# First pair of feature tiles of each FFN by plain products, and what goes with it

## The chip, the cores and the metric

The kernel runs on one core of a Trainium2 chip. Its time is the device time of one execution in microseconds (us). The kernel before takes 1070.05 us, the median of 3 runs (1069.14 to 1070.71).

## The reference

One layer of a streaming encoder on a sequence of 512 positions, 1024 features, in float32:

```
x = x + 0.5 * swiglu(rms_norm(x, ffn1_norm), w_gate1, w_up1, w_down1)     # FFN 1
x = x + mixer(rms_norm(x, mix_norm))                                      # SSD scan and chunked attention
x = x + 0.5 * swiglu(rms_norm(x, ffn2_norm), w_gate2, w_up2, w_down2)     # FFN 2
return rms_norm(x, final_norm)
# swiglu(h, g, u, d) = (silu(h @ g) * (h @ u)) @ d ; g, u: 1024 x 2816, d: 2816 x 1024
```

The change touches the two FFNs (and one buffer of the attention).

## The kernel before

Everything lies transposed: features on the 128 partitions, the 512 positions on the free axis. x is 8 tiles of 128 x 512, the 2816 inner features are 22 tiles, taken in 11 pairs. Each float32 product is made of three TensorE matmuls on operands that are split in a high and a low part (high x high, high x low, low x high); ScalarE (ACT) makes the high part of a weight tile and VectorE (DVE) the low one (`usplit`, lines 284 and 286).

Gate and up of one pair are computed together by a scheme of seven products in place of eight (the Strassen-Winograd kind): `wgu[d, 0..3]` are four blocks of weights (gate and up, each over four of the eight input tiles, 512 KB a block), x has four quarters (input tiles 0 to 3 and 4 to 7, positions LO = 0 to 255 and HI = 256 to 511), and the products P1 to P7 take a block or a sum of blocks by a quarter or a sum of quarters. One product is a *unit*: 2 feature tiles x 4 input tiles x 3 = 24 matmuls of 256 columns (line 445). P1, P2 and P4 take plain weights. P5, P6, P3 and P7 take sums of blocks, which the DMAs make: P5's buffer is loaded with block 2 by a plain DMA (line 318) and block 3 is added by an accumulating DMA that GpSimd (POOL) issues (line 321); after P5's split block 0 is added for P6, after that split block 1 for P3. For P7 block 2 is added onto P1's buffer. So a pair takes four plain and four accumulating loads of 512 KB. The buffer of sums, `view(d)`, exists twice (tile s40), that of plain weights, `raw`, four times.

The sums of x (`XCombos`) are made on DVE: `weigh` multiplies x by the norm weights into `xw`, `sum1`, `sums23` and `sum4` make the sums, `parts1`, `parts23`, `parts4` split them in high and low; `base` splits plain x.

1/rms isn't in x: it is put in after the products. `rstd_begin` sums squares (accumulated in `acc` by `add_squares`, square on ACT, add on DVE line 170) over partitions with ones matmuls and runs some 15 tiny DVE operations; `rstd_both` spreads the result to all partitions with two matmuls and copies it to `rs[0]` (1/rms) and `rs[1]` (-0.5/rms). After P3, gate is multiplied by `rs[0]`, then SiLU, then by up (after P4), and the product is split for the down matmul. The down matmul's output is multiplied by `rs[1]` and added to x (`add`, lines 483 and 484).

The order of the work is written out in `program()`: units of pairs 0 and 1 interleaved, then for d = 2 to 10: P5(d), P1(d), P3(d-1), P4(d-1), P6(d), P2(d), P7(d), and after pairs 4 and 8 a block of down matmuls ("D"), the third block at the end. After each unit one step of a generator (`early1`, `early2`) does a piece of the sums of x and of 1/rms. `ws.get()` hands out the weights: it splits `look` units ahead and starts the DMAs of the next 8 units by the lead that each one has. The instructions of each engine run in an order fixed at compile time; a scheduler may place an instruction earlier than the text does when its inputs and buffers are free in its own reckoning, and the text's order is its priority. Each engine, and each queue that issues DMAs (SP, POOL), runs its own list in order.

In the attention four tiles `kz0` to `kz3` of 128 x 512 hold a part of the keys. In FFN 2 the last three output tiles are finished by halves of the positions (`last2`).

Of the kernel before, what the change touches and what calls it, by code (L numbers as in the profile page):

```python
# [38 lines left out]
def hybrid_block(ctx: ExitStack, tc, xT, par, wgu1, wd1, win, wdt, wv, wo, rbt, wgu2, wd2, out):  # L39
# [83 lines left out]
    class Stream:  # L123
# [40 lines left out]
    def add_squares(acc, src, first):  # L164
# [72 lines left out]
    GROUPS = {22: 8, 36: 4, 40: 4, 44: 4}  # L237
# [63 lines left out]

    def ffn_weights(wgu, wd, n_last=0):
# [20 lines left out]
        for step in program(n_last):  # L323
            if step[0] == "P":
# [3 lines left out]
                if p == "P1":  # L328
# [28 lines left out]
    class XCombos:  # L357


        def __init__(self, wcol):  # L360
# [3 lines left out]
            self.b1, self.t1 = [[two() for _ in range(2)] for _ in range(2)]  # L364
            self.b2, self.t23 = [[two() for _ in range(4)] for _ in range(2)]
# [35 lines left out]
        def split(self, dst, src):  # L401
            d = [p.rearrange("p (a b) -> p a b", a=2) for p in dst]
# [15 lines left out]
        def moving(self, p, k):
            if p == "P1":
                return self.half(self.b1, k)  # L420
            if p == "P5":
                return self.half(self.t1, k)
            if p == "P4":
                return self.half(self.t4, k)
            t, h = {"P2": (self.b2, LO), "P3": (self.b2, HI), "P6": (self.t23, HI), "P7": (self.t23, LO)}[p]
            return [a[:, h] for a in t[k]]

    def ffn(xc, early, after, last=None, n_last=0):
# [4 lines left out]
        early = early(rs)  # L433

        def run(p, d):
# [22 lines left out]
            elif p == "P3":  # L458
                V.tensor_tensor(out=e["b"], in0=e["H"], in1=e["b"], op=ALU.add)
                e["s"] = []  # L460
                for t, h in (("a", LO), ("b", HI)):
# [3 lines left out]
                    S.activation(out=s, in_=e[t], func=AF.Silu)  # L465
                    e["s"].append(s)
            elif p == "P4":

                q = HSLOT[d % 4]
                th, tl = [wide_tile(group(q))[:, i - group(q):i - group(q) + 2] for i in (q, q + 2)]  # L470
# [6 lines left out]
                for j in range(2):  # L477
                    hh[2 * d + j], hl[2 * d + j] = th[:, j], tl[:, j]
                del st[d]

        def add(o, ps):
            t = sb("fh", [P, SEQ], bufs=2)
            V.tensor_tensor(out=t, in0=ps, in1=rs[1], op=ALU.mult)  # L483
            V.tensor_tensor(out=x[:, o], in0=x[:, o], in1=t, op=ALU.add)

        pss = {}
        for i, step in enumerate(program(n_last)):
            if step[0] == "P":
                run(*step[1:])
                next(early, None)  # L490
# [40 lines left out]
    for k in range(4):  # L531
        xc1.base(x[:, k], k)
# [8 lines left out]

    def early1(rs):
        ws.look = 2
# [3 lines left out]
        for k in range(4):  # L547
            xc1.weigh(x[:, k], k)
        yield
        ws.look = 3  # L550
        xc1.sum1()
        xc1.parts1()
        for k in range(4, 8):
            xc1.weigh(x[:, k], k)
        yield
        xc1.sums23()
        yield
        for k in range(4):
            xc1.parts23(k)
        yield  # L560
        acc = sb("acc", [P, SEQ])
        for k in range(4):
            add_squares(acc, x[:, k], k == 0)
        yield
        xc1.sum4()
        xc1.parts4()
        for k in range(4, KD):
            add_squares(acc, x[:, k], False)
        dg, _ = rstd_begin(acc, D)
        yield  # L570
# [3 lines left out]
        yield  # L574
        rstd_both(rs, dg)
# [222 lines left out]
    def do_qk(j, n, ps):  # L798
# [260 lines left out]
    for o in range(KD):  # L1059
# [7 lines left out]
        if o < 4:  # L1067
            xc3.weigh(x[:, o], o)
        add_squares(accs[1], x[:, o], o == 0)
        if o == 4:  # L1070
            xc3.sum1()
        if o >= 5:
            xc3.weigh(x[:, o - 1], o - 1)

    def early2(rs):
        xc3.weigh(x[:, KD - 1], KD - 1)
        yield
        xc3.parts1()
        yield
        xc3.sums23()  # L1080
        yield
        for k in range(4):
            xc3.parts23(k)
        yield
        dg, _ = rstd_begin(accs[1], D)
        yield
        xc3.sum4()
        xc3.parts4()
        yield
        yield  # L1090
        rstd_both(rs, dg)
        yield
# [12 lines left out]
    def last2(hh, hl, rsm):  # L1105
# [115 lines left out]
```

## Time and profile before

| | us |
|---|---|
| median of 3 runs | 1070.05 |
| the profiled execution | 1071.2 |
| its span | 1069.5 |
| granted TensorE clock, mean | 0.987 |

In the profile, PE is the matmul engine, PEld its weight loads, DVE VectorE, ACT ScalarE, POOL GpSimd, SP the queue that issues plain DMAs. A row of the timeline has the start, the duration, the engine, the line of the kernel, the operation, output and input tiles, shapes, the number of merged instructions, and in brackets the idle time before it and what ended it. A row of groups has count, busy us and mean ns of one, then the idle time before and its releasers.

### The profile page before, as it was taken

What the parts mean: (1) busy time and instruction counts of PE and PEld (TensorE: products, weight loads), DVE (VectorE), ACT (ScalarE), POOL (GpSimd) and SP (SyncE); (2) the same over time, 40 slices, a digit from 0 to 9 for tenths busy, and PEclk for the clock granted to TensorE, in tenths of its full rate; (3) what the DMA queues carried; (4) which work ended last, traced back from release to release, by engine and by line L of the source; (5) the groups of instructions that cost most, each with busy time, mean ns of one, the idle gap of its engine ahead of it and who ended that gap; (6) DMA issues with size and microseconds to landing.
All of it is one profiled execution on the core that took longest, in us unless ns stands there. A gap on an engine that the chain in (4) does not pass through costs nothing.

```text
span 1069.5 us, 16508 instructions
## 1 busy us (share of the span) xinstructions
PE 1027.5 (96%) x6494; PEld 923.7 (86%) x6494; DVE 760.4 (71%) x1252; ACT 551.1 (52%) x876; POOL 137.0 (13%) x157
## 2 busy tenths in 40 slices
PE   7799999999999999999999999998899999999995
PEld 6799889998899877878888778888898899989985
DVE  6787655675466878988867999787675477645765
ACT  6565432563244546755666876656462155423543
POOL 2111100110010003323201111110110011100000
PEclk9799999999999999999999999999999999999997
DMA  9789754986453322222232232757895388853612
GB/s 300 155 178 220 199 136 104 212 223 172 118 113 95 118 76 73 79 60 78 60 99 80 79 99 80 181 114 170 203 237 140 99 183 210 219 134 98 137 46 79
DMA packets 44126, 145.92 MB, mean 136 GB/s; under 512 B 4624, under 2 KB 7952, under 8 KB 44048
## 3 DMA queue, kind: packets, MB, share of 16 engines
q1 hardware_dynamic: 29136, 95.69, 26.7%
q0 software_dynamic: 12672, 46.14, 25.1%
q10 hardware_dynamic: 2240, 3.02, 1.0%
q8 instruction: 51, 0.84, 0.3%
q14 instruction: 27, 0.22, 0.1%
HBM read 142.74 MB, written 2.10 MB: 135 GB/s over the span
## 4 chain that ended last, share of the span: by engine, by line
PE 66%; DMA 11%; DVE 11%; issue 6%; ACT 5%; POOL 0%; SPq 0%; DVEq 0%; ACTq 0%; POOLq 0%
PE mm L445 16%; PE mm L154 12%; PE mm L155 12%; PE mm L156 12%; PE aux L445 10%; DMA s<-wgu 10%; DVE fs L625 2%; DVE xw L286 2%; ACT xw L284 2%; DVE wlo L104 1%; PE aux L985 1%; PE aux L749 0%; DMA raw<-wd 0%; ACT s L475 0%; PE aux L1007 0%
## 5 line engine op out<-in xcount | busy, mean ns | idle before, releaser
L445 PE MATMUL mm<-s,xw 128*128 128x256 f32 x2112 | 272.8, 287 | 16.1 <-ACT fu L453 8.2
L445 PEld LDWEIGHTS mm<-s,xw 128*128 128x128 f32 x2112 | 264.4, 196 | 19.7 <-ACT fu L453 9.5
L445 PE MATMUL aux<-s,xw 128*128 128x256 f32 x1584 | 202.7, 285 | 8.1 <-ACT xw L284 6.6
L445 PEld LDWEIGHTS aux<-s,xw 128*128 128x128 f32 x1584 | 196.5, 193 | 9.5 <-ACT xw L284 6.8
L102 ACT CAST whi<-raw 128x512 fp32r<-128x512 f32 (+1 forms) x178 | 105.9, 603 | 154.7 <-PE mm L155 126.6
L104 DVE TENSOR_TENSOR wlo<-raw,whi 128x512 fp32r<-128x512 f32 (+1 forms) x178 | 122.5, 694 | 48.5 <-ACT whi L102 47.6
L286 DVE TENSOR_TENSOR xw<-raw,xw 128x1024 fp32r<-128x1024 f32 x88 | 107.5, 1221 | 52.1 <-ACT xw L284 52.0
L155 PE MATMUL mm<-s,whi 128*128 128x512 f32 x366 | 142.7, 390 | 0.0
L154 PE MATMUL mm<-s,whi 128*128 128x512 f32 x366 | 142.5, 390 | 0.0
L156 PE MATMUL mm<-s,wlo 128*128 128x512 f32 x366 | 142.4, 389 | 0.0
L284 ACT CAST xw<-raw 128x1024 fp32r<-128x1024 f32 x88 | 92.1, 1048 | 89.4 <-PE mm L445 35.6
L284 ACT CAST xw<-s 128x1024 fp32r<-128x1024 f32 x66 | 69.1, 1048 | 132.6 <-PE aux L445 53.9
L286 DVE TENSOR_TENSOR xw<-s,xw 128x1024 fp32r<-128x1024 f32 x66 | 80.6, 1221 | 54.9 <-ACT xw L284 54.8
L154 PE MATMUL mm<-xw,whi 128*128 128x512 f32 x288 | 118.0, 410 | 0.0
L321 POOL DMA_DIRECT2D s<-wgu x66 | 57.8, 892 | 456.6 <-DVE xw L286 288.8
L155 PE MATMUL mm<-xw,whi 128*128 128x512 f32 x288 | 113.0, 392 | 0.0
L156 PE MATMUL mm<-xw,wlo 128*128 128x512 f32 x288 | 112.8, 392 | 0.0
L155 PEld LDWEIGHTS mm<-s,whi 128*128 128x128 f32 x366 | 68.7, 188 | 14.4 <-DVE s L476 0.4
L154 PEld LDWEIGHTS mm<-s,whi 128*128 128x128 f32 x366 | 68.7, 188 | 14.3 <-ACT s L1011 0.2
L156 PEld LDWEIGHTS mm<-s,wlo 128*128 128x128 f32 x366 | 68.7, 188 | 14.3
L483 DVE TENSOR_TENSOR fh<-mm,rstd 128x512 f32<-128x512 f32 x45 | 31.0, 689 | 59.8 <-PE mm L156 59.7
L154 PEld LDWEIGHTS mm<-xw,whi 128*128 128x128 f32 x288 | 54.1, 188 | 12.0 <-issue 2.2
(250 smaller groups left out, 1298.3 us busy)
## 6 DMA issues: line engine op xcount, KB each, us to landing
raw<-wgu SPq DMA_DIRECT2D x66, 512.0 KB, 4.4
s<-wgu POOLq DMA_DIRECT2D x66, 512.0 KB, 5.8
raw<-wd SPq DMA_DIRECT2D x32, 512.0 KB, 4.8
raw<-win SPq DMA_DIRECT2D x28, 512.0 KB, 3.5
s<-wgu SPq DMA_DIRECT2D x22, 512.0 KB, 5.0
raw<-wgu POOLq DMA_DIRECT2D x22, 512.0 KB, 6.0
raw<-wd SPq DMA_DIRECT2D x16, 384.0 KB, 3.3
raw<-wo SPq DMA_DIRECT2D x12, 512.0 KB, 3.6
```

Of the source, the lines that this page charges most:

```text
L102: S.copy(out=hi, in_=src)
L104: V.tensor_tensor(out=lo, in0=src, in1=f(hi), op=ALU.subtract)
L154: T.matmul(ps, lhsT=sh, rhs=mh, start=start, stop=False, skip_group_check=skip)
L155: T.matmul(ps, lhsT=sh, rhs=ml, start=False, stop=False, skip_group_check=skip)
L156: T.matmul(ps, lhsT=sl, rhs=mh, start=False, stop=stop, skip_group_check=skip)
L284: S.copy(out=hi, in_=src)
L286: V.tensor_tensor(out=lo, in0=src, in1=f(hi), op=ALU.subtract)
L321: return lambda: G.dma_start(out=get(), in_=src, accum_op=ALU.add)
L445: T.matmul(ps[:, j * HS:(j + 1) * HS], lhsT=sw[:, j, k], rhs=m, start=(p in ("P1", "P2", "P5") and j == 0 and k == 0 and n == 0), stop=(k ...
L483: V.tensor_tensor(out=t, in0=ps, in1=rs[1], op=ALU.mult)
L625: V.scalar_tensor_tensor(out=y[:, d:SEQ], in0=u[:, 0:SEQ - d], scalar=cw(j), in1=y[:, d:SEQ], op0=ALU.mult, op1=ALU.add)
L985: T.transpose(out=pp[:, kt * P:(kt + 1) * P], in_=pr[:, kt * P:(kt + 1) * P], identity=ident)
```

## The change

- Pair 0 of each FFN is computed without the scheme: four units A11, A21 (input tiles 0 to 3 by gate, by up) and A12, A22 (input tiles 4 to 7), each of 24 matmuls of 512 columns, added up in four PSUM tiles (two of three "mm", two of five "aux") that are held until 1/rms is there (`plain_end`). The order is A11(0), A21(0), A12(0), P5(1), P1(1), A22(0), P6(1), P2(1), P7(1), then d = 2 to 10 as before. The pieces of the sums of x follow these units, for both FFNs by one generator; in FFN 2 `weigh` and `sum1` move from the loop of the output projection to there.
- `b1` holds whole tiles of plain x; `parts1` writes the split sum over their HI half when A21 is done.
- Four buffers for weight sums (tiles s40 and s52), so P5 of pair d waits for P3 of pair d - 4; leads 10 and 7 in place of 8 and 6, and DMAs are looked at 12 units ahead. The memory is that of `kz0` to `kz3`, which are now four slots of s52.
- `rs[1]` is multiplied into SiLU(gate) (two halves a pair), and `add` is one DVE operation; the same in `last2`.
- The adds of squares for 1/rms of both FFNs go from DVE to GpSimd.
- The start: x comes in whole tiles, the first unit's weights in two halves, and its splits alternate with those of x.

```diff
-            for n in range(self.done, min(len(self.jobs), i + 9)):
+            for n in range(self.done, min(len(self.jobs), i + 12)):
...
-            V.tensor_tensor(out=acc, in0=acc, in1=sq, op=ALU.add)
+            (eng or V).tensor_tensor(out=acc, in0=acc, in1=sq, op=ALU.add)
...
-    GROUPS = {22: 8, 36: 4, 40: 4, 44: 4}
+    GROUPS = {22: 8, 36: 4, 40: 4, 44: 4, 52: 4}
...
-        out = [("P", p, d) for p, d in (("P1", 0), ("P1", 1), ("P2", 0), ("P2", 1), ("P5", 0), ("P5", 1), ("P6", 0),
-                                        ("P6", 1), ("P7", 0), ("P7", 1), ("P3", 0), ("P4", 0))]
+        out = [("P", p, d) for p, d in (("A11", 0), ("A21", 0), ("A12", 0), ("P5", 1), ("P1", 1), ("A22", 0), ("P6", 1),
+                                        ("P2", 1), ("P7", 1))]
...
-                bufs[d] = wide_tile(40, F32)[:, 2 * (d % 2):2 * (d % 2) + 2].rearrange("p a (k c) -> p a k c", c=P)
+                t = wide_tile((40, 52)[d // 2 % 2], F32)[:, 2 * (d % 2):2 * (d % 2) + 2]
+                bufs[d] = t.rearrange("p a (k c) -> p a k c", c=P)
...
-                    j = Job(lambda d=d: usplit(view(d)), (8, jobs.get(("P3", d - 2)), first(d)),
-                            (6, None, more(sum_, A[3])))
+                    j = Job(lambda d=d: usplit(view(d)), (10, jobs.get(("P3", d - 4)), first(d)),
+                            (7, None, more(sum_, A[3])))
...
+        def plain(p):
+            if not st:
+                st["A1"], st["A2"] = [mmps(), mmps()], [aux(), aux()]
+            wh, wl = ws.get()
+            for k in range(4):
+                for j in range(2):
+                    mm3(st["A" + p[1]][j], wh[:, j, k], wl[:, j, k], *xc.moving(p, k), p[2] == "1" and k == 0,
+                        p[2] == "2" and k == 3)
+
+        def plain_end():
+            th, tl = h_tiles(0)
+            for j in range(2):
+                a = sb("fa", [P, SEQ], bufs=3)
+                V.tensor_tensor(out=a, in0=st["A1"][j], in1=rs[0], op=ALU.mult)
+                s = sb("fs", [P, SEQ], bufs=2)
+                S.activation(out=s, in_=a, func=AF.Silu)
+                V.tensor_tensor(out=s, in0=s, in1=rs[1], op=ALU.mult)
+                h = sb("fh", [P, SEQ], bufs=2)
+                V.scalar_tensor_tensor(out=h, in0=st["A2"][j], scalar=-1.0, in1=s, op0=ALU.mult, op1=ALU.mult)
+                S.copy(out=th[:, j], in_=h)
+                V.tensor_tensor(out=tl[:, j], in0=h, in1=f(th[:, j]), op=ALU.subtract)
+            del st["A1"], st["A2"]
...
                     S.activation(out=s, in_=e[t], func=AF.Silu)
+                    s3 = s.rearrange("p (j a) -> p j a", j=2)
+                    V.tensor_tensor(out=s3, in0=s3, in1=rs[1][:, h].unsqueeze(1).broadcast_to([P, 2, HS]), op=ALU.mult)
...
         def add(o, ps):
-            t = sb("fh", [P, SEQ], bufs=2)
-            V.tensor_tensor(out=t, in0=ps, in1=rs[1], op=ALU.mult)
-            V.tensor_tensor(out=x[:, o], in0=x[:, o], in1=t, op=ALU.add)
+            V.tensor_tensor(out=x[:, o], in0=x[:, o], in1=ps, op=ALU.add)
...
-    for k in (0, 2):
-        nc.sync.dma_start(out=x[:, k:k + 2, LO], in_=xT[:, k:k + 2, LO])
-    ws.jobs[0].move(0, True)
+    raw0 = sb("raw", [P, 2, 4, P], bufs=4)
+    for n in range(2):
+        nc.sync.dma_start(out=x[:, 2 * n], in_=xT[:, 2 * n])
+        nc.sync.dma_start(out=raw0[:, :, 2 * n:2 * n + 2], in_=wgu1[0, 0, :, :, 2 * n:2 * n + 2])
+        nc.sync.dma_start(out=x[:, 2 * n + 1], in_=xT[:, 2 * n + 1])
...
+    def early(xc, rs, acc, squares):
+        for k in range(KD):
+            xc.weigh(x[:, k], k)
+        xc.sum1()
+        ws.look = max(ws.look, 2)
+        yield
+        xc.parts1()
+        squares(range(0, 4))
+        ws.look = 3
+        yield
+        xc.sums23()
+        for k in range(4):
+            xc.parts23(k)
+        squares(range(4, KD))
+        yield
+        dg, _ = rstd_begin(acc, D)
+        yield
+        xc.sum4()
+        yield
+        rstd_both(rs, dg)
+        yield True
+        xc.parts4()
+        yield
...
-            t = [slot(i) for i in sl[2:]] + [sb(f"kz{j}", [P, SEQ], F32R)]
+            t = [slot(i) for i in sl[2:]] + [slot(52 + j)]
...
-        if o < 4:
-            xc3.weigh(x[:, o], o)
-        add_squares(accs[1], x[:, o], o == 0)
-        if o == 4:
-            xc3.sum1()
-        if o >= 5:
-            xc3.weigh(x[:, o - 1], o - 1)
+        add_squares(accs[1], x[:, o], o == 0, G)
```

## Rows read from the trace of the kernel before

**Rows 1.** The page, part 1: busy us, share of the span, instructions.
```profile
PE 1027.5 (96%) x6494; PEld 923.7 (86%) x6494; DVE 760.4 (71%) x1252; ACT 551.1 (52%) x876; POOL 137.0 (13%) x157
```

**Rows 2.** Windows: length, busy PE, PEld, DVE, ACT, POOL, then PEclk, DMA share, GB/s.
```profile
7.63:126.38 118.75, 105.24 (x802) 102.89 (x803) 89.87 (x120) 69.94 (x99) 21.10 (x26) 0.94 0.87 213
24.00:48.00 24.00, 14.29 (x77) 13.31 (x78) 15.83 (x19) 10.99 (x15) 4.30 (x5) 0.72 0.85 165
697.36:806.05 108.69, 99.48 (x802) 98.03 (x803) 81.48 (x114) 61.27 (x84) 15.70 (x18) 0.98 0.78 183
...
130.00:330.00 200.00, 200.00 (x1341) 185.60 (x1340) 118.98 (x152) 80.71 (x110) 18.98 (x22) 1.00 0.62 151
```

**Rows 3.** Waits of PE, 0 to 130 us: total us, times, longest.
```profile
PE aux L445 <- ACT xw L284: 6.6, 1, 6.6
PE mm L445 <- ACT xw L284: 4.0, 2, 2.0
PE mm L445 <- ACT fu L453: 1.8, 1, 1.8
```

**Rows 4.** Timeline at the start and at the first weight sum.
```profile
4.44 1.74 ACT L161 ACTIVATE s<-x,par 128x256 fp32r<-128x256 f32 x4 [1.56 <-DMA x<-xT]
...
7.63 0.80 PE L445 MATMUL mm<-s,xw 128*128 128x256 f32 x2 [1.94 <-ACT xw L284]
...
29.60 0.80 PE L445 MATMUL aux<-s,xw 128*128 128x256 f32 x2 [6.57 <-ACT xw L284]
```

**Rows 5.** Timeline of PE at full clock: two units, and matmuls of 512 columns.
```profile
783.01 3.04 PE L445 MATMUL mm<-s,xw 128*128 128x256 f32 x24
785.89 3.04 PE L445 MATMUL aux<-s,xw 128*128 128x256 f32 x24
...
808.12 0.39 PE L154 MATMUL mm<-s,whi 128*128 128x512 f32 x1
...
808.80 0.39 PE L154 MATMUL mm<-s,whi 128*128 128x512 f32 x1
```

**Rows 6.** Timeline of PE in the head of FFN 2, two rows with waits.
```profile
729.93 0.47 PE L217 MATMUL aux<-s,onesr 128*128 128x512 f32 x1 [1.47 <-DVE s L210]
...
761.52 4.38 PE L445 MATMUL mm<-s,xw 128*128 128x256 f32 x24 [4.28 <-ACT fu L453]
```

**Rows 7.** Timeline of the queues: first sums' plain loads issued, first accumulation.
```profile
6.53 0.86 SPq L318 DMA_DIRECT2D s<-wgu  x2
...
21.54 0.85 POOL L321 DMA_DIRECT2D s<-wgu  x1 [6.76 <-DMA s<-wgu]
```

**Rows 8.** The page, part 3: packets, MB, share of 16 engines' span.
```profile
q1 hardware_dynamic: 29136, 95.69, 26.7%
q0 software_dynamic: 12672, 46.14, 25.1%
```

**Rows 9.** Groups of DVE by shape, 0 to 130 us.
```profile
L286 DVE TENSOR_TENSOR xw<-s,xw 128x1024 fp32r<-128x1024 f32 x16 | 19.6, 1223 | 18.2 <-ACT xw L284 18.2
...
L170 DVE TENSOR_TENSOR acc<-acc,fh 128x512 f32<-128x512 f32 x7 | 4.8, 682 | 0.0
...
L162 DVE SCALAR_TENSOR_TENSOR s<-x,par,s 128x512 fp32r<-128x512 f32 x4 | 2.9, 746 | 0.0
```

**Rows 10.** Groups of POOL by shape, whole span.
```profile
L680 POOL TENSOR_TENSOR fh<-dt,tri 128x512 fp32r<-128x512 f32 x16 | 21.3, 1333 | 18.2 <-DVE acc L170 18.2
```

**Rows 11.** Line 384 by itself: ns min/median/max.
```profile
L384 DVE TENSOR_SCALAR s<-x,par x8: 473/480/1470, 8.8 to 706.5; 128x512 f32<-128x512 f32 x8
```

**Rows 12.** Timeline of POOL at 13 us.
```profile
13.46 1.32 POOL L816 MEMSET kz<- 64x512 f32 x2
```

**Rows 13.** The page, part 5: the multiplication by 1/rms after the down matmul.
```profile
L483 DVE TENSOR_TENSOR fh<-mm,rstd 128x512 f32<-128x512 f32 x45 | 31.0, 689 | 59.8 <-PE mm L156 59.7
```

**Rows 14.** Timeline of DVE at the last pair of FFN 1 and at the end.
```profile
343.90 0.69 DVE L473 TENSOR_TENSOR fh<-mm,fs 128x512 f32<-128x512 f32 x1 [1.46 <-PE mm L445]
...
1057.15 0.41 DVE L1126 TENSOR_TENSOR fs<-mm,rstd 128x256 f32<-128x256 f32 x1
```

More of the change, by code (lines that the diff above doesn't have):

```diff
@@ L162, in split_act, with add_squares @@
         V.scalar_tensor_tensor(out=lo, in0=src, scalar=wcol, in1=f(hi), op0=ALU.mult, op1=ALU.subtract)
-    def add_squares(acc, src, first):
+    def add_squares(acc, src, first, eng=None):
         if first:
@@ L327, in ffn_weights @@
                 A = wgu[d]
-                if p == "P1":
+                if p[0] == "A":
+                    n = ("A11", "A12", "A21", "A22").index(p)
+                    j = Job(lambda p=p: usplit(bufs[p]), (5, None, plain(p, A[n])))
+                elif p == "P1":
                     j = Job(lambda d=d: usplit(bufs["g", d]), (5, None, plain(("g", d), A[0])))
@@ L363, in __init__ @@
             two = lambda: (slot(next(it)), slot(next(it)))
-            self.b1, self.t1 = [[two() for _ in range(2)] for _ in range(2)]
-            self.b2, self.t23 = [[two() for _ in range(4)] for _ in range(2)]
+            self.b1, self.b2, self.t23 = [[two() for _ in range(4)] for _ in range(3)]
             self.xw = wide_tile(22, F32)
@@ L399, in sum4, with split @@
                                    op1=ALU.subtract)
-        def split(self, dst, src):
-            d = [p.rearrange("p (a b) -> p a b", a=2) for p in dst]
+        def split(self, d, src):
             S.copy(out=d[0], in_=src)
@@ L406, in parts1, with two @@
         def parts1(self):
-            for i in range(2):
-                self.split(self.t1[i], self.xw[:, 2 * i:2 * i + 2, LO])
+            for k in range(4):
+                self.split([p[:, HI] for p in self.b1[k]], self.xw[:, k, LO])
+        def two(self, dst):
+            return [p.rearrange("p (a b) -> p a b", a=2) for p in dst]
         def parts23(self, k):
-            self.split(self.t23[k], self.xw[:, k::4, HI])
+            self.split(self.two(self.t23[k]), self.xw[:, k::4, HI])
         def parts4(self):
@@ L488, in ffn @@
             if step[0] == "P":
-                run(*step[1:])
-                next(early, None)
+                if step[1][0] == "A":
+                    plain(step[1])
+                else:
+                    run(*step[1:])
+                if next(early, None):
+                    plain_end()
                 continue
@@ L504, in ffn @@
             a, b = 2 * BLOCKS[2][0], 2 * BLOCKS[2][1]
-            last([hh[k] for k in range(a, b)], [hl[k] for k in range(a, b)], rs[1])
+            last([hh[k] for k in range(a, b)], [hl[k] for k in range(a, b)])
     x2, accs = [], []
@@ L530, in hybrid_block, with first_unit @@
     xc1 = XCombos(C_F1)
-    for k in range(4):
-        xc1.base(x[:, k], k)
+    def first_unit():
+        turn[0] = 1
+        hi, lo = [sb(f"xw{i}", [P, 2, 4, P], F32R) for i in range(2)]
+        for n in range(2):
+            xc1.base(x[:, 2 * n], 2 * n)
+            k = slice(2 * n, 2 * n + 2)
+            S.copy(out=hi[:, :, k], in_=raw0[:, :, k])
+            V.tensor_tensor(out=lo[:, :, k], in0=raw0[:, :, k], in1=f(hi[:, :, k]), op=ALU.subtract)
+            xc1.base(x[:, 2 * n + 1], 2 * n + 1)
+        return hi, lo
+    ws.jobs[0] = Job(first_unit)
     def rstd_both(rs, dg):
@@ L540, in rstd_both @@
             rs.append(r)
+    def early(xc, rs, acc, squares):
[9 more added lines that the diff above has]
+        xc.sums23()
+        for k in range(4):
+            xc.parts23(k)
[9 more added lines that the diff above has]
+        yield
     def early1(rs):
-        ws.look = 2
         for k in range(4, 8):
@@ L546, in early1 @@
         yield
[L547 to L560, printed above, removed]
-        acc = sb("acc", [P, SEQ])
[L562 to L570, printed above, removed]
+        acc = sb("acc", [P, SEQ])
+        yield from early(xc1, rs, acc, lambda ks: [add_squares(acc, x[:, k], k == 0, G) for k in ks])
         S.copy(out=dw[:, :, 0:16], in_=dtw)
@@ L1066, in hybrid_block @@
         xc3.base(x[:, o], o)
-        if o < 4:
-            xc3.weigh(x[:, o], o)
-        add_squares(accs[1], x[:, o], o == 0)
-        if o == 4:
-            xc3.sum1()
-        if o >= 5:
-            xc3.weigh(x[:, o - 1], o - 1)
+        add_squares(accs[1], x[:, o], o == 0, G)
     def early2(rs):
-        xc3.weigh(x[:, KD - 1], KD - 1)
         yield
[L1078 to L1092, printed above, removed]
+        yield from early(xc3, rs, accs[1], lambda ks: None)
     def after2(o):
```

40 lines of the change are left out of this document (17 added, 23 removed).

## The prediction

> **What bounds the kernel now.** I read the page's busy line first, and the reader is to see TensorE at 96% of the span [rows 1]: time can only be won where PE stands still or runs slowly, and whatever adds matmuls costs at once. Next the windows view, stretch by stretch. From 130 to 330 us PE is busy 200.00 of 200.00 us at full clock [rows 2]. The heads of the two FFNs are different: 7.63 to 126.38 (FFN 1, first product to first down matmul) is 118.75 us long, 697.36 to 806.05 (FFN 2, the same stretch) is 108.69 us.
>
> What should they take? A unit (one product of one pair, 24 matmuls of 256 columns) goes from 783.01 to 785.89, 2.88 us [rows 5]. Both heads hold 33 units (seven for each of pairs 0 to 4, less P3 and P4 of pair 4): 95.0 us, and I put 1.4 us for the ten matmuls of 1/rms, an estimate (eight of one column, two of 512 columns at 0.23 us, below). So 96.4 us without a stall, and **22.3 us are lost in head 1, 12.3 us in head 2**.
>
> The waits view of PE names the causes. In the first 130 us the longest wait is 6.6 us on an ACT split of a weight sum, then 4.0 us on two more [rows 3]; the 6.6 us are the wait before 29.60, the first product that needs a sum [rows 4]. The rest of head 1's loss is clock: 24 to 48 us was granted 0.72 of full speed [rows 2], after PE had waited. So a removed wait gives back more than its length. In head 2 one wait of 4.28 us stands before 761.52 and one of 1.47 us for 1/rms before 729.93 [rows 6].
>
> Why are sums late? A sum is a plain load and then an accumulating load onto it. The queue totals give the rates: q1 moved 95.69 MB in 26.7% of 1069.5 us (335 GB/s), q0, which accumulates, 46.14 MB in 25.1% (172 GB/s) [rows 8]; so 512 KB cost 1.56 us plain and 3.05 us accumulated. A pair by seven products takes four of each, 18.4 us of transfers for 20.2 us of PE: hardly any slack, and at the start x (2.1 MB) and four weight loads stand in front. The first sum's plain load was issued at 6.53 and landed only at 21.54, when the accumulation could be issued [rows 7].
>
> **The change part by part.**
>
> Plain products. Pair 0 becomes 4 loads with 96 matmuls of 512 columns. Three such take 808.80 - 808.12 = 0.68 us [rows 5], so 96 x 0.227 = 21.8 us against 7 x 2.88 = 20.2: **+1.6 us a FFN, +3.2 in all**, all on the path. It removes four accumulations and no plain load: 4 x 3.05 = 12.2 us of transfers at the worst place. The three plain units ahead of the first sum give 16.3 us of PE work that need 1.57 MB.
>
> Start. x arrives as whole tiles and the first unit's weights in two halves. The first ACT pass over x starts at 4.44 now [rows 4]; it would start near there again, then one pass of x (0.7 us) and one half of the weights (0.6 us) come before the first matmul, near 5.8, with about 0.5 us lost on the first low parts (0.75 us, L162 [rows 9], and 0.68). Against 7.63 [rows 4] that is -1.3 us; bounds 0 and -1.8.
>
> When is the next thing late? With PE from 6.3, the first sum (P5 of pair 1) is needed at 6.3 + 16.3 = 22.6. Before it 3.7 MB go through q1 (11 us), then its own two transfers, 4.6 us; with 3.6 us before the first bytes (256 KB of x, 0.8 us, are there at 4.44 [rows 4]) it would land at 19 alone, and I take 21, since other loads share the engines. Split: 1.05 us on ACT, 1.22 on DVE [rows 9]. So it is on time or some 1 us late. DVE has to fit much into the same 17 us: three splits (3.7), eight low parts of x (6.0) [rows 9], the two halves (1.4), weights on x (4 x 0.48) [rows 11], a sum (1.2), parts1 (about 1.7, an estimate from the 0.41 us of a 256-column pass [rows 14]): 16 us. It fits with nothing to spare, so I expect stalls of 1 to 3 us here and as much when the parts for P6 follow.
>
> Sums into four buffers, issued earlier. This takes the wait on P3 of two pairs before away. It moves no byte less. Where the sums are already in time (130 to 330) it brings nothing; in head 2 the next pairs can be fetched while the output projection runs, and the 4.28 us wait should go. In head 1 the same freedom lets the loads and accumulations of pairs 2 to 4 enter the queues ahead of those that pair 1 still needs, up to 3 x 4.6 = 13.8 us of transfers. Bounds: no harm, or 13.8 us plus clock. I take 4 us.
>
> 1/rms of up into h. It drops one of two DVE passes per finished output (L483, 45 of 689 ns, plus the small ones of the last block [rows 13]) and adds two 512-column passes to each of 20 pairs: 27.6 us more against 31.0 us less on DVE. On the path the dropped pass counts only at the very end: the 0.41 us at 1057.15 stand between the last product and the squares [rows 14], **-0.4 us**. The added ones lie beside PE: DVE is busy 118.98 of 200.00 us in 130 to 330 [rows 2]. At the last pair, where h is wanted at once, DVE idles 1.46 us before 343.90 [rows 14], and 0.69 fits. I take 0; if DVE were full it would be up to 1.4 us a pair.
>
> Squares on GpSimd. 7 adds a FFN leave DVE, 7 x 0.685 = 4.8 us [rows 9]. A GpSimd add of this shape is shown only with a broadcast operand, 1.33 us [rows 10]; seven take 9.3 us, and accumulating transfers are issued on the same engine, in order, so adds may wait behind one that waits for its load. 1/rms is wanted when pair 0's psum has to be freed, at about 42 us in head 1; acc would be done near 32 and 1/rms 10 us later. I take 1 us a FFN; bounds 0 and 9.3.
>
> The same adds may also slow DVE. The row first: a DVE pass of 480 ns took 1470 at most, and that was beside GpSimd memsets at the start [rows 11, 12]. The Trainium skill (GPSIMD Engine Reference, 8. Key points) says that GpSimd shares its SBUF interfaces with VectorE and contends with DVE instructions of two SBUF inputs, which the splits are. By that rule the adds take up to 14 x 1.33 = 18.6 us from DVE and the sum below would end near 1066; by the row I leave the 1 us.
>
> The sum, against the profiled execution (1071.2 us, span 1069.5): lost now 22.3 + 12.3 = 34.6; left over 7.5 in head 1 (2 at the first sums, 4 run-ahead, 1.5 for 1/rms and clock) and 3 in head 2; plain products +3.2; start -1.3; tail -0.4. 34.6 - 10.5 - 3.2 + 1.3 + 0.4 = 22.6, so 1048.6. The median shown lies 1.15 below the profiled execution: **1047.5 us**.
>
> **The rivals.**
> *Run-ahead.* Early loads for pairs 2 to 4 hold up A22 and the sum of P6 in head 1: 10 us more stalls and slow clock than forecast, **1058**. For it: the first sum of before took 15.0 us to land amid other loads [rows 7]. Against: pair 0 now needs 12.2 us less. The skill's page DMA: Bandwidth & Descriptors (Queues, rings and completion order) has each DMA engine take the queues in turn by packets, so an accumulation for later takes its share from a load for now; by that the time is this rival's, and the 15.0 us agree.
> *Nearly no stall.* Left over is 2 us in all: 1047.5 - 8.5 = **1039**. For it: head 1 would have 19 plain weight loads (29.7 us), 15 accumulations (45.8), x (6.3) and four down loads (6.2), 88 us of transfers in the 104 that end a head without stalls. Against: ACT and DVE work in order, and a split that waits for a transfer holds a copy that PE needs, as before 761.52.
> *GpSimd adds exposed.* 14 x 1.33 = 18.6 us, as late 1/rms or as DVE time: **1066**. For it the 1470 ns; against, that half of them lie where PE has plain work ready.
> *Slower: the scaling of h.* Two more DVE passes stand between P3 and h in each of 20 pairs. If DVE and ACT become what sets the pair, 20 x 1.38 = 27.6 us come back: 1047.5 + 27.6 = **1075**. It decides from 22.6 us on, that is with over four fifths of it exposed. Against: PE has no gap in 130 to 330 with DVE at 59%.
>
> **How the numbers follow.** Forecast 0.55 (own range 1042 to 1054), run-ahead 0.17, nearly no stall 0.14, GpSimd adds 0.08, scaling of h 0.06. The range 1038 to 1060 takes in the first three almost whole. About 0.2% can be told from no change. Faster holds all cases but the last; of that I give 0.02 to no change, and 0.05 to slower.
>
> **What would show it.** Right: first matmul near 6; no wait over 3 us in head 1 and clock at 1.00 by 50 us; the first down matmul at 106 to 113 instead of 126.38, and FFN 2's head at 99 to 103 us instead of 108.69; waits before 761.52 gone; 130 to 330 still without a gap. The run-ahead shows as ACT waiting for DMA before P6 or A22 of FFN 1 with the clock below 1 behind it; the GpSimd adds as PE waiting for the ones matmuls or for a psum; the scaling as PE waiting on ACT or DVE in every pair. A head 1 that still ends after 120, or gaps between the pairs, would make the prediction wrong.

## The result and the profile after

The changed kernel takes **1058.5 us** (median of 4 runs, 1056.37 to 1060.4) against 1070.09 of the kernel before (4 runs): ratio 0.9892, interval 0.9871 to 0.9912, 11.6 us less. The forecast was 22.6 us less. One of the four runs of e6 below (1252.12 us, at a granted clock of 0.75) is a slow one and is left out of its median. The page of after, its busy line (part 1) and its two big queues (part 3), beside [rows 1] and [rows 8]:

```profile
PE 1026.2 (97%) x6350; PEld 915.2 (87%) x6350; DVE 757.1 (72%) x1224; ACT 547.2 (52%) x869; POOL 150.1 (14%) x163
...
q1 hardware_dynamic: 29040, 95.69, 27.2%
q0 software_dynamic: 11520, 41.95, 22.5%
```

144 matmuls and 4.2 MB of accumulated loads are gone as the diff says, and GpSimd has 13 us more. The windows of after (columns as in [rows 2]): head 1 to the first down matmul, its 24 to 48 us, the pairs behind it, head 2 alone.

```profile
6.84:118.60 111.76, 103.84 (x730) 97.92 (x731) 96.59 (x122) 67.47 (x100) 27.25 (x27) 0.95 0.89 234
24.00:48.00 24.00, 17.10 (x89) 15.25 (x89) 22.42 (x23) 12.59 (x20) 9.84 (x9) 0.82 0.93 205
130.00:328.00 198.00, 198.00 (x1349) 184.75 (x1348) 118.58 (x152) 83.18 (x113) 18.31 (x23) 1.00 0.56 140
694.91:794.13 99.22, 98.72 (x730) 94.22 (x731) 81.56 (x112) 57.78 (x81) 17.48 (x18) 1.00 0.70 168
```

Head 2 is 99.22 us and the pairs are still without a gap. Head 1 ends at 118.60 instead of 126.38, and in 24 to 48 us DVE is busy 22.42 of 24 us, 15.83 before [rows 2]. The span cut by what TensorE does; the last column is the best of the later experiments (us, worked out from the times of PE's matmuls in the profiled executions, whose spans are 13.1 us apart):

| stage | before | after | change | forecast | e10 |
|---|---|---|---|---|---|
| start and head 1, to its last product | 126.50 | 118.72 | -7.8 | -14.5 | 114.09 |
| rest of FFN 1 and mixer, to the last transpose | 547.03 | 546.47 | -0.6 | 0 | 546.64 |
| output projection, to FFN 2's first product | 23.83 | 29.72 | **+5.9** | 0 | 24.13 |
| head 2 | 108.81 | 99.34 | -9.5 | -7.7 | 98.13 |
| rest | 263.32 | 262.17 | -1.1 | -0.4 | 262.59 |

So two places are to be explained: head 1, and the output projection ahead of head 2, which the forecast had not in its sum at all. Head 1 first: waits of PE, 0 to 125 us (columns as in [rows 3]).

```profile
PE aux L479 <- ACT xw L284: 3.5, 1, 3.5
PE aux L479 <- DVE s L405: 2.4, 2, 1.2
PE aux L198 <- POOL acc L170: 1.1, 1, 1.1
PE aux L217 <- DVE s L210: 0.9, 1, 0.9
```

The timelines of after around that first wait, one engine after the other (SP and POOL issue the loads; then ACT, DVE, PE):

```profile
7.62 0.43 SPq L320 DMA_DIRECT2D s<-wgu  x1
...
10.90 0.43 SPq L320 DMA_DIRECT2D s<-wgu  x1
...
16.39 1.43 POOL L170 TENSOR_TENSOR acc<-acc,fh 128x512 f32<-128x512 f32 x1 [13.74 <-ACT fh L169]
17.77 1.00 POOL L323 DMA_DIRECT2D s<-wgu  x1
...
26.40 1.04 ACT L284 CAST xw<-s 128x1024 fp32r<-128x1024 f32 x1 [1.79 <-DMA s<-wgu]
...
28.62 3.72 DVE L405 TENSOR_TENSOR s<-s,s 128x256 fp32r<-128x256 f32 x4
...
32.27 3.02 DVE L286 TENSOR_TENSOR xw<-raw,xw 128x1024 fp32r<-128x1024 f32 x1
...
6.84 0.50 PE L154 MATMUL mm<-s,xw 128*128 128x512 f32 x1 [1.22 <-ACT xw L574]
...
27.50 0.38 PE L479 MATMUL aux<-s,xw 128*128 128x256 f32 x1 [3.46 <-ACT xw L284]
29.09 2.13 PE L479 MATMUL aux<-s,xw 128*128 128x256 f32 x9 [1.21 <-DVE s L405]
```

The first sum's accumulation is issued at 17.77, behind an add on the same engine, and its split starts at 26.40: 8.6 us for what [rows 8] put at 3.05. Behind it DVE takes 3.72 us for four passes of 256 columns and 3.02 for a low part that was 1.22 [rows 9].

Then the output projection. Timelines of after: SP, ACT, POOL, DVE, PE.

```profile
667.58 0.33 SPq L320 DMA_DIRECT2D s<-wgu  x1
668.01 0.81 SPq L316 DMA_DIRECT2D raw<-wgu  x1
...
678.84 1.05 ACT L284 CAST xw<-raw 128x1024 fp32r<-128x1024 f32 x1 [3.92 <-DMA raw<-wgu]
...
666.14 0.90 POOL L323 DMA_DIRECT2D s<-wgu  x1 [13.46 <-DMA s<-wgu]
667.54 0.88 POOL L323 DMA_DIRECT2D s<-wgu  x1 [0.50 <-issue]
...
681.29 3.83 POOL L170 TENSOR_TENSOR acc<-acc,fh 128x512 f32<-128x512 f32 x2
...
680.55 0.75 DVE L162 SCALAR_TENSOR_TENSOR s<-x,par,s 128x512 fp32r<-128x512 f32 x1 [3.94 <-ACT s L161]
681.22 2.78 DVE L286 TENSOR_TENSOR xw<-raw,xw 128x1024 fp32r<-128x1024 f32 x1
683.92 1.75 DVE L162 SCALAR_TENSOR_TENSOR s<-x,par,s 128x512 fp32r<-128x512 f32 x1
...
686.19 0.67 DVE L1112 TENSOR_TENSOR x<-x,mm 128x512 f32<-128x512 f32 x1
...
687.01 0.47 PE L154 MATMUL mm<-s,whi 128*128 128x512 f32 x1 [3.09 <-DVE x L1112]
```

Read it backwards. PE waits 3.09 for a psum that DVE empties late (L1112); DVE was late twice. First it stood 3.94 us because ACT, which works in order, waited 3.92 for a block of weights that took 10.8 us from its issue. That block is not one of the output projection's: it belongs to FFN 2's first pair (`raw` from `wgu`), and its split stands in ACT's list among the splits of x. Two accumulations and the load of one sum had been issued in the 2 us ahead of it, and another sum's load followed 0.9 us later. Then two passes took 4.53 instead of 1.97 while GpSimd added. Theory: both new liberties, early loads and adds on GpSimd, cost this. Rivals: early loads alone; the adds alone, by slowing DVE; or the extra DVE passes of the scaling of h.

### The profile page after: what moved, and what is told of

The parts are those of the page before. It is cut to its first block, busy times and chain, and to the rows that moved or that the text cites. A ratio compares the mean times of both kernels' runs of the same rounds, so it can differ in the third digit from the quotient of the medians.

```text
span 1056.4 us, 16176 instructions
## 1 busy us (share of the span) xinstructions
PE 1026.2 (97%) x6350; PEld 915.2 (87%) x6350; DVE 757.1 (72%) x1224; ACT 547.2 (52%) x869; POOL 150.1 (14%) x163
## 3 DMA queue, kind: packets, MB, share of 16 engines
q10 hardware_dynamic: 2240, 3.02, 0.9%
## 5 line engine op out<-in xcount | busy, mean ns | idle before, releaser
L479 PE MATMUL mm<-s,xw 128*128 128x256 f32 x1920 | 242.2, 284 | 0.0
L479 PEld LDWEIGHTS mm<-s,xw 128*128 128x128 f32 x1920 | 236.8, 193 | 0.2
L479 PE MATMUL aux<-s,xw 128*128 128x256 f32 x1440 | 185.7, 285 | 6.2 <-ACT xw L284 3.5
L479 PEld LDWEIGHTS aux<-s,xw 128*128 128x128 f32 x1440 | 180.0, 194 | 8.0 <-ACT xw L284 3.9
L104 DVE TENSOR_TENSOR wlo<-raw,whi 128x512 fp32r<-128x512 f32 (+1 forms) x178 | 122.4, 692 | 55.6 <-ACT whi L102 55.1
L286 DVE TENSOR_TENSOR xw<-raw,xw 128x1024 fp32r<-128x1024 f32 x87 | 109.7, 1261 | 43.8 <-ACT xw L284 43.1
L284 ACT CAST xw<-s 128x1024 fp32r<-128x1024 f32 x60 | 62.8, 1047 | 101.5 <-PE aux L479 61.4
L323 POOL DMA_DIRECT2D s<-wgu x60 | 52.9, 905 | 402.6 <-DVE xw L286 256.9
L286 DVE TENSOR_TENSOR xw<-s,xw 128x1024 fp32r<-128x1024 f32 x60 | 73.2, 1220 | 27.0 <-ACT xw L284 27.0
L514 DVE TENSOR_TENSOR x<-x,mm 128x512 f32<-128x512 f32 x45 | 30.9, 687 | 74.6 <-PE mm L156 74.6
```

The lines of the kernel that those rows point to most:

```text
L104: V.tensor_tensor(out=lo, in0=src, in1=f(hi), op=ALU.subtract)
L284: S.copy(out=hi, in_=src)
L286: V.tensor_tensor(out=lo, in0=src, in1=f(hi), op=ALU.subtract)
L323: return lambda: G.dma_start(out=get(), in_=src, accum_op=ALU.add)
L479: T.matmul(ps[:, j * HS:(j + 1) * HS], lhsT=sw[:, j, k], rhs=m, start=(p in ("P1", "P2", "P5") and j == 0 and k == 0 and n == 0), stop=(k ...
L514: V.tensor_tensor(out=x[:, o], in0=x[:, o], in1=ps, op=ALU.add)
```

## The experiments

Each is the changed kernel with the edit shown. All were timed in several rounds beside the kernel before (1068.87 us for e1 to e4, 1069.52 for e5 to e8, 1068.89 for e9 and e10). The changed kernel was not timed again beside them, and before was 1070.09 beside it, so a difference to 1058.5 is sure to about 1 us only: e1, 5.9 us less by the medians, is 4.6 us less by the ratios. "Out-proj" is the third stage of the table, from the one profiled run of each.

| | median us | ratio, interval | head 1 | out-proj | head 2 |
|---|---|---|---|---|---|
| after | 1058.5 | 0.9892, 0.9871-0.9912 | 118.72 | 29.7 | 99.3 |
| e1 squares on DVE | 1052.62 | 0.9849, 0.9836-0.9861 | 115.78 | 26.3 | 99.5 |
| e2 two sums | 1051.0 | 0.9833, 0.9821-0.9846 | 115.85 | 25.3 | 99.4 |
| e3 scale at end | 1059.42 | 0.9915, 0.9902-0.9928 | 119.11 | 29.3 | 99.3 |
| e4 held loads | 1056.73 | 0.988, 0.9864-0.9896 | 119.78 | 24.3 | 102.9 |
| e5 = e4 + e1 | 1053.89 | 0.9858, 0.9843-0.9873 | 121.76 | 24.0 | 98.1 |
| e6 = e2 + e1 | 1054.81 | 0.9864, 0.9847-0.988 | 122.15 | 24.1 | 98.1 |
| e7 e1 in FFN 2 only | 1055.3 | 0.9864, 0.9848-0.9881 | 118.73 | 27.4 | 99.5 |
| e8 21 more adds | 1058.5 | 0.9897, 0.9882-0.9912 | 118.03 | 29.9 | 99.3 |
| e9 = e1 + held, FFN 2 | 1049.22 | 0.9815, 0.9797-0.9834 | 116.51 | 24.1 | 98.1 |
| e10 = e9 + held, FFN 1 | **1047.29** | 0.9796, 0.9777-0.9814 | 114.09 | 24.1 | 98.1 |

**e1: the adds back on DVE.**

```diff
-            (eng or V).tensor_tensor(out=acc, in0=acc, in1=sq, op=ALU.add)
+            V.tensor_tensor(out=acc, in0=acc, in1=sq, op=ALU.add)
```

> The changed kernel with one part undone: the squares are added on DVE again in both FFNs. Theory A (the adds on GpSimd slow DVE: a splitting pass of 1.22 us took 2.78 and 3.02 beside one, a pass of 0.75 us took 1.75 five times): DVE gets back some 14 x 1.0 us and loses 14 x 0.68, its passes are 0.75 and 1.22 us again everywhere, the 3.25 us stall of the output projection goes and head 1 loses 3 us less, in all 1050 to 1053. It also expects the first accumulation to be issued at 15.8 (when its load has landed) and not at 17.77 behind an add. Theory B (run-ahead transfers alone): DVE is not what is late, 14 adds return to it, 1058 to 1061.

5.9 us less, though DVE got 14 passes more. Groups of DVE by shape, 670 to 700 us, first of after, then of e1 (columns as in [rows 9]):

```profile
L162 DVE SCALAR_TENSOR_TENSOR s<-x,par,s 128x512 fp32r<-128x512 f32 x7 | 9.3, 1332 | 3.9 <-ACT s L161 3.9
L1112 DVE TENSOR_TENSOR x<-x,mm 128x512 f32<-128x512 f32 x8 | 5.4, 678 | 0.9 <-PE mm L156 0.9
L286 DVE TENSOR_TENSOR xw<-raw,xw 128x1024 fp32r<-128x1024 f32 x2 | 4.0, 2001 | 1.1 <-ACT xw L284 1.1
...
L386 DVE TENSOR_SCALAR s<-x,par 128x512 f32<-128x512 f32 x3 | 2.5, 832 | 0.1
```

```profile
L162 DVE SCALAR_TENSOR_TENSOR s<-x,par,s 128x512 fp32r<-128x512 f32 x8 | 6.0, 747 | 4.4 <-ACT s L161 4.4
L1112 DVE TENSOR_TENSOR x<-x,mm 128x512 f32<-128x512 f32 x8 | 5.4, 681 | 0.9 <-PE mm L156 0.9
L170 DVE TENSOR_TENSOR acc<-acc,fh 128x512 f32<-128x512 f32 x7 | 4.8, 686 | 0.0
...
L286 DVE TENSOR_TENSOR xw<-raw,xw 128x1024 fp32r<-128x1024 f32 x2 | 2.4, 1218 | 0.0
...
L386 DVE TENSOR_SCALAR s<-x,par 128x512 f32<-128x512 f32 x4 | 1.8, 484 | 0.0
```

L162 and L286 fall back to the 746 and 1223 of [rows 9]. L386, which has one input tile, falls back too, from 832 to 484. L1112, one of whose inputs is PSUM, was never slow, but in after none of its passes here ran beside an add, so only e8 below tells whether it would be. The wait of ACT on the weights is still there (4.4 of DVE's idle time behind it), so e1 parts the two causes in the output projection. In head 1 the first accumulation, with no add in front of it, was issued at 16.16 instead of 17.77, yet its split began at 25.75 instead of 26.40: the place behind an add cost 0.65 us there. **e7: only FFN 2's adds back on DVE.**

```diff
-        add_squares(accs[1], x[:, o], o == 0, G)
+        add_squares(accs[1], x[:, o], o == 0)
```

> The changed kernel with only FFN 2's squares back on DVE; FFN 1's stay on GpSimd. It parts the 5.9 us of the full undoing by place. From the stage times (output projection and head 2 lost 3 us in the changed kernel that the undone one did not, head 1 the rest): 1055 to 1056.5, head 1 as in the changed kernel (first down matmul near 118.6), the output projection's 3.25 us stall before 687 at most 1.5.

Head 1 stayed at 118.73, and the 3.2 us were gained behind it: the adds cost about the same in each FFN.

**e2: two buffers of sums again**, with the leads of before.

```diff
-            for n in range(self.done, min(len(self.jobs), i + 12)):
+            for n in range(self.done, min(len(self.jobs), i + 9)):
...
-                t = wide_tile((40, 52)[d // 2 % 2], F32)[:, 2 * (d % 2):2 * (d % 2) + 2]
+                t = wide_tile(40, F32)[:, 2 * (d % 2):2 * (d % 2) + 2]
...
-                    j = Job(lambda d=d: usplit(view(d)), (10, jobs.get(("P3", d - 4)), first(d)),
-                            (7, None, more(sum_, A[3])))
+                    j = Job(lambda d=d: usplit(view(d)), (8, jobs.get(("P3", d - 2)), first(d)),
+                            (6, None, more(sum_, A[3])))
```

> The changed kernel with two buffers of weight sums and the leads of before; the rest of the change stays. Theory B (with four buffers the loads of pairs 2 to 4 share the engines with what pair 1 needs): the first sum lands by 22 instead of 26.4, the 3.46 us wait before 27.50 goes to under 1 us, and the weights split at 678.84 in the output projection land some 4 us earlier; the later heads lose a little again to sums that come late (up to 4 us as before at 761.52): 1052 to 1058. Theory A: stalls stay where DVE is slow, and the missing buffers cost: 1059 to 1065.

7.5 us less, 2.9 in head 1 and 4.4 in the output projection: the four buffers, with their leads, are a loss as they stand.

**e6: both undone**, the edits of e1 and e2 together.

> The changed kernel with both undone: two buffers of weight sums and the squares on DVE; plain first pair, order, start and scaling of h stay. If the two losses are separate (adds on GpSimd 5.9 us, run-ahead 7.5 us, both measured against the 1058.5 of the changed kernel), 1045 to 1047. If they are the same lost time found twice (whichever goes first gives it all back), 1050 to 1052.

The output projection and head 2 gain 6.8 together, but head 1 ends at 122.15, later than by either edit alone. Waits of e6's SP, 45 to 80 us, then its timeline, POOL and ACT, and last ACT's row at the same place of e2:

```profile
SPq L320 <- DVE xw L286: 6.6, 1, 6.6
...
62.30 1.76 POOL L323 DMA_DIRECT2D s<-wgu  x2 [14.21 <-DVE xw L286]
...
74.28 1.04 ACT L284 CAST xw<-s 128x1024 fp32r<-128x1024 f32 x1 [8.74 <-DMA s<-wgu]
...
67.93 1.05 ACT L284 CAST xw<-s 128x1024 fp32r<-128x1024 f32 x1 [1.75 <-DMA s<-wgu]
```

With two buffers SP waits 6.6 us for one to come free and loads pair 3's first sum from 59.34 only. Its accumulation is the second of the two in the POOL row (issued at 63.15; the 14.21 us before the first are a wait for the split of another sum) and lands 11.0 us later, and PE stands 5.3 us for a copy that is stuck behind the split. e2 has the same two buffers: there the buffer came free at 57.55, this accumulation went out first of the two, at 61.48, ACT waited 1.75 us and PE not at all. So two buffers need not cost this. With the adds on DVE head 1 is 6.4 us shorter with four buffers (e1) than with two (e6), with the adds on GpSimd 2.9 longer (after against e2); why the order of the two accumulations turned was not tested.

**e4, e5: four buffers, but the loads of pairs 2 to 4 held** until the first sum has been split, by a one-element write into their buffer; e5 has the adds on DVE too.

```diff
+                    after_ = jobs["P5", 1] if d in (2, 3, 4) else jobs.get(("P3", d - 4))
+                    def go(d=d, fn=first(d)):
+                        if d in (2, 3, 4):
+                            V.tensor_copy(out=view(d)[:, 0, 0, 0:1], in_=f(jobs["P5", 1].parts[1][:, 0, 0, 0:1]))
+                        fn()
...
+                    j = Job(lambda d=d: usplit(view(d)), (10, after_, go), (7, None, more(sum_, A[3])))
```

> The changed kernel with four buffers, but the first plain loads of pairs 2 to 4 of each FFN have to wait until pair 1's first sum has been split (a DVE pass of one element writes into each of these buffers first and reads the split). Theory B: the first sum of FFN 1 lands by 22 to 23 instead of 26.4 and the wait before 27.50 falls from 3.46 to under 1.5; in the output projection the ACT wait of 3.92 before 678.84 goes; the kernel gains 3 to 6 us, 1052 to 1055. Theory A: the add on GpSimd still holds the first accumulation until 17.77 and DVE stays slow, so 1 to 2 us at most: 1056 to 1058.

> Four buffers with the first loads of pairs 2 to 4 held back until pair 1's first sum has been split, and the squares on DVE. Held back alone gave 1056.7, with PE waiting 4.18 us for the squares at 42.65, which stood on POOL behind accumulations that were waiting for those loads. Theory: with the squares off POOL nothing waits behind a held load, so that wait goes and the kernel lands at 1047 to 1050, near two buffers with squares on DVE. Rival: held loads are late themselves (the sums of pairs 2 to 4 bunch up), 1051 to 1055.

In head 1 this failed (119.78 and 121.76). e4's waits of PE, 0 to 125 us, have a new first row,

```profile
PE aux L198 <- POOL acc L170: 4.0, 1, 4.0
```

and the timelines of e4 (POOL, then ACT) show what the last add waited for:

```profile
27.70 0.85 POOL L323 DMA_DIRECT2D s<-wgu  x1 [0.25 <-ACT fh L169]
...
41.17 1.43 POOL L170 TENSOR_TENSOR acc<-acc,fh 128x512 f32<-128x512 f32 x1 [0.28 <-ACT fh L169]
...
37.36 1.05 ACT L284 CAST xw<-s 128x1024 fp32r<-128x1024 f32 x1 [3.55 <-DMA s<-wgu]
...
40.40 0.62 ACT L169 ACTIVATE fh<-x 128x512 f32<-128x512 f32 x1
```

It waited for its square, which ACT made at 40.40, behind the split of pair 1's second sum, and for that sum ACT had stood 3.55 us. Its accumulation, issued at 27.70, took 9.6 us to land, beside the held loads, which were let go from 27.83 on; in e2, which has no such loads there, it was issued at 27.66 and took 5.3. So it was not, as the expectation of e5 says, that adds stood behind accumulations waiting for held loads: the held loads came at a bad moment for pair 1. In e5 the longest wait of PE is for 1/rms (3.1 us before 55.23), and the granted clock behind it was 0.71 and 0.69 (48 to 56 and 56 to 64 us); no wait there is for a sum of pair 2.

Behind the mixer holding helped: output projection and head 2 take 127.2 together in e4 and 122.1 in e5, 129.1 in after. In e4 the output projection is as short as in e5, with the adds still on GpSimd, and the loss has moved: PE waits 2.9 us for DVE in head 2's first unit.

**e9, e10: adds on DVE; loads of pairs 2 to 4 held in FFN 2** (e9), and of pairs 3 and 4 in FFN 1 as well (e10); the code of e4 with its pairs in a list. The code is e9's; in e10 the list for FFN 1 is (3, 4) instead of ().

```diff
+        GD = (2, 3, 4) if n_last else ()
...
+                    after_ = jobs["P5", 1] if d in GD else jobs.get(("P3", d - 4))
```

> Squares on DVE, four buffers; the first loads of pairs 2 to 4 are held back in FFN 2 only. By place, from the stage times of the runs so far: head 1 as with squares on DVE alone (first down matmul at 115.8), the output projection and head 2 as with both undone (from the last transpose of the attention to the end of head 2's products 122.1 us, against 129.1 in the changed kernel and 125.8 with squares on DVE alone): 1048 to 1050. If holding back in one FFN changes nothing there and the gain of the earlier run was a matter of order alone: 1052 to 1054.

> The same, and in FFN 1 the first loads of pairs 3 and 4 are held back too, pair 2's not. With nothing but pair 2's load beside it, the first accumulation of FFN 1 should land by 23 instead of 25.7 and PE's wait of 2.35 before the first sum go to under 1, while pair 2's sum is not late as it was when its load was held back as well (head 1 ended at 121.8 there): head 1 at 113 to 115, in all 1045 to 1048. Rival: the held loads bunch up behind it and head 1 ends at 117 or later, 1050 or more.

e10 is the best version, 1047.29 us, 11.2 less than after. Its only wait of PE from 640 to 720 us, and its windows at 24 to 48 and from 660 to 702:

```profile
PE mm L154 <- ACT s L1065: 0.5, 1, 0.5
```

```profile
24.00:48.00 24.00, 18.89 (x115) 17.22 (x116) 20.26 (x34) 14.16 (x20) 4.02 (x5) 0.89 0.78 167
660.00:702.00 42.00, 41.49 (x188) 34.00 (x187) 38.68 (x61) 26.44 (x44) 5.24 (x6) 1.00 0.72 185
```

The output projection is back at 24.1 us, before's 23.8. In head 1 the first sum is still late: its waits of PE, 0 to 125 us,

```profile
PE aux L486 <- ACT xw L284: 2.1, 1, 2.1
PE mm L486 <- ACT fu L494: 1.4, 1, 1.4
```

where I had expected under 1 us. The sum itself lands at 24.9, 26.4 in after.

**e3: the scaling of h undone**, rs[1] multiplied in behind the down matmul as in the kernel before.

```diff
-                    s3 = s.rearrange("p (j a) -> p j a", j=2)
-                    V.tensor_tensor(out=s3, in0=s3, in1=rs[1][:, h].unsqueeze(1).broadcast_to([P, 2, HS]), op=ALU.mult)
...
-            V.tensor_tensor(out=x[:, o], in0=x[:, o], in1=ps, op=ALU.add)
+            t = sb("fh", [P, SEQ], bufs=2)
+            V.tensor_tensor(out=t, in0=ps, in1=rs[1], op=ALU.mult)
+            V.tensor_tensor(out=x[:, o], in0=x[:, o], in1=t, op=ALU.add)
```

> The changed kernel with 1/rms of up put in after the down matmul again, as before. Both theories: DVE has time beside PE in the pairs, so this moves only the end (+0.4 us) and leaves the pairs without gaps: 1058 to 1060. If the two passes a pair are what the gain was lost to, it is under 1054.

1059.42 against 1058.5, within the 1 us above; in its profile the stretch with the dropped pass, from the last product of FFN 2 to the end, takes 47.1 us, 45.6 in after. In the pairs the scaling is off the path: PE is busy 198.00 of 198.00 us from 130 to 328 in both.

**e8: does an add slow DVE wherever it lies?** 21 adds on GpSimd whose sum nobody reads, in the units of pairs 5 to 7 of FFN 1.

```diff
+            if xc is xc1 and 5 <= d <= 7:
+                if "dm" not in probe:
+                    probe["dm"] = sb("acc", [P, SEQ])
+                    G.tensor_tensor(out=probe["dm"], in0=x[:, 0], in1=x[:, 1], op=ALU.add)
+                else:
+                    G.tensor_tensor(out=probe["dm"], in0=probe["dm"], in1=x[:, 1], op=ALU.add)
```

> The changed kernel with 21 more GpSimd adds of 128x512 (x plus a spare tile) right after the first down block of FFN 1, in the stretch 162 to 200 us where PE has no gap and nothing else runs on GpSimd but accumulations. It measures the disputed cost by itself. If an add stops DVE's passes of two SBUF inputs for about 1 us, the splits (1.22 us) show 2.2 to 2.8 us beside an add, DVE fills up in that stretch and PE shows gaps: 3 to 12 us slower than 1058.5. If the long passes of DVE were something else (waits for transfers), splits stay at 1.22 us and the time at 1058 to 1059.

No time was lost (1058.5); I had the place wrong, since the adds ran early, at 130 to 163 us, beside the first down block. There the groups of DVE by shape, 120 to 162 us, of after and of e8:

```profile
L104 DVE TENSOR_TENSOR wlo<-raw,whi 128x512 fp32r<-128x512 f32 x12 | 8.3, 688 | 8.2 <-ACT whi L102 8.2
...
L514 DVE TENSOR_TENSOR x<-x,mm 128x512 f32<-128x512 f32 x7 | 4.8, 688 | 13.4 <-PE mm L156 13.4
```

```profile
L104 DVE TENSOR_TENSOR wlo<-raw,whi 128x512 fp32r<-128x512 f32 x12 | 13.6, 1143 | 5.9 <-ACT whi L102 5.9
...
L521 DVE TENSOR_TENSOR x<-x,mm 128x512 f32<-128x512 f32 x8 | 5.5, 685 | 12.6 <-PE mm L156 12.6
```

The same passes go from 688 to 1143 ns, those with PSUM stay, and the idle time before them pays for it. Six of the eight passes with PSUM ran beside an add here and took 674 to 689 ns. So the slowing follows the adds, not the stage, and it cost nothing where DVE had idle time.

## Why the prediction was right and wrong

**Right:** plain products at their price (e10's head 2, without a wait, took 98.1 us where the sum has 98.0) and head 2 at 99 to 103 (99.22); the wait before 761.52 gone; first matmul at 6.84 (near 6 was said, with 0.5 lost behind it); 130 to 330 without a gap; the scaling of h at nothing (e3), which refutes the slower rival; a tail of -0.4 can't be told from none (from the last product of FFN 2 to the end it measured -0.57, from 46.2 to 45.6 us, and e1, e2 and e4 to e10 took 45.3 to 46.4). Two signs failed: PE waited 3.46 us in head 1, where none over 3 was said, and the first down matmul came at 118.60, not at 106 to 113; from 48 to 56 us the granted clock was still 0.89.

**Wrong, step 1: "Squares on GpSimd ... I take 1 us a FFN".** It measured 5.9 us for both by the medians (e1), 4.6 by the ratios. The bound above it, 9.3 a FFN, held. I weighed the one 1470 ns row [rows 11] beside memsets too low; the Trainium skill (GPSIMD Engine Reference, 8. Key points) has GpSimd contend with DVE instructions of two SBUF inputs or in a 2-port perf mode, and on the first the traces agree: 746 to 1332 ns for L162, 688 to 1143 for L104, 674 to 689 beside an add with a PSUM input (e8). By that rule 18.6 us were to go; less did, and e8 shows adds that cost no time where DVE had some to spare. L386, with one input tile, was slowed too, from 0.48 to 1.52 us; no run here shows in which mode it ran. In head 1 "it fits with nothing to spare" was right, and for that reason the 1 us could not be.

**Wrong, step 2: "in head 2 the next pairs can be fetched while the output projection runs".** I booked the gain and no cost. The fetch ran ahead of weights of FFN 2's first pair whose split stands on ACT before passes that the output projection waited for (10.8 us from issue to landing); two buffers take 4.4 us from that stage (e2), held loads alone 5.5, of which 3.5 come back in head 2 (e4), held loads and DVE adds together 5.6 (e9). The run-ahead that I had looked for in head 1 alone acts here as well. The Trainium skill (DMA: Bandwidth & Descriptors, Queues, rings and completion order) has each DMA engine take the queues in turn, so that accumulations for later take their share. The 10.8 us agree, with two accumulations and a sum's load issued in the 2 us ahead; in e9, which holds those loads back, the plain weight loads issued from 656 to 680 us landed after 3.4 to 4.9.

**Head 1's stalls.** Without a stall it takes 96.4 + 1.6 = 98.0 us; from the first product on it took 111.9 in after, 13.9 lost where I had left 7.5. The row of 6.84 to 118.60 parts them: PE idle for 7.9 us and busy for 103.84, 5.8 more than 98.0, which I put down to the clock (0.95 on average); I had 1.5 for the clock and 1/rms together. e10 loses 107.6 - 98.0 = 9.6. So 4.3 of the 6.4 too many are early loads and adds; the rest is the first sum, late in every version (2.08 before 26.03 in e10), and the clock behind it, 0.82 in after and 0.89 in e10. I had this sum landing at 21; it landed at 26.4 in after and at 24.5 to 25.9 in the versions looked at (e1, e2, e4 to e6, e9, e10), though its plain load was there by 16.1 in all of them. So it was the accumulation: 6.5 to 9.7 us from issue to landing, where I had the mean rate's 3.05 and little more. The run-ahead was taken at 4 us: undoing it alone gave 2.9, with another wait in its place. That the effects don't add (2.9 and 2.9 alone, a loss together in e6) is shown; how far head 1 could come by a better order of its loads was not tried further.

The changed kernel came out at the time of the run-ahead rival (1058), but by a mixture: of the 11.2 us that e10 wins back, undoing the adds gave 5.9 first (e1) and holding the loads the other 5.3, holding alone, with pair 2 of FFN 1 held too, gave 1.8 (e4); and half of the 11.2 lies in the output projection (5.6), where the rival had nothing. My own range of 1042 to 1054 missed, and the wider one held only because it took in that rival. That e10's 1047.29 is so near the 1047.5 forecast is partly chance: head 2 with the output projection came out 2.7 us better than forecast, head 1 2.1 worse.

## What to carry to other kernels

More buffers are leave to load early, and an in-order issuer takes it at once: ask of each load that may now go sooner which urgent one it will pass, hold it by a dependency until that one has landed, and ask again what it will meet when it is let go. Work given to an idle engine is not free when it slows a neighbour's passes: price it in those, as far as something waits for them, and look at the DMA issues that stand behind it. Sum the stages ahead of the one you are changing as well, since early work lands there.

## What the runs showed of the hardware

- A GpSimd add of 128x512 f32 with both inputs in SBUF took 1.28 to 1.30 us beside nothing (e8) and 1.35 to 2.14 in after. A DVE pass with two SBUF inputs that an add slowed took 1.75 to 2.57 us in after instead of 0.68 to 0.75 (128x512), and 2.78 and 3.02 instead of 1.22 (128x1024). A pass with one input tile (L386) took 1.52 instead of 0.48. A pass with one PSUM input took the same (674 to 689 ns, e8).
- Every slowed pass of after and e8 ended at a set time behind the end of an add, wherever in the add it had begun: 0.55 to 0.56 us at 128x512, 1.08 to 1.09 at 128x1024, 0.28 for L386. So a pass loses what is left of the add that it meets. Of the passes that began just before an add some were slowed in this way and some took their usual time.
- An accumulating load of 512 KB at the start took 8.6 us from issue to landing in after, where the mean rate gives 3.05.
- After the wait of 3.09 us before 687.01, TensorE's matmuls of 512 columns came every 0.23 us for 1.4 us; the next seven, from 688.37, came every 0.43 us, 3 us in all at a granted clock of 0.50 (1.2 instead of 2.4 GHz).
